# Moving 21 of 24 merge gates into the delta-net and state-space stages of a hybrid block, with convolutions in chunks and chain instructions put ahead

## The chip, the cores and the metric

The kernel runs on one core of a Trainium2 chip. The metric is the device time in microseconds of one execution. TensorE (PE) multiplies matrices and writes to PSUM; VectorE (DVE), ScalarE (ACT) and GpSimd (POOL) work on elements; SyncE (SP) issues most of the DMAs. Each engine takes its instructions in the order in which they stand in its own queue, and waits at an instruction until its inputs are there and its output buffer is free.

## The reference, cut to what matters

The kernel computes one layer of a hybrid block on 1024 tokens (plus 16 learned ones put in front, so T = 1040) and a model width of 1024. Three branches read the same normed input; three gates, each as wide as the model, weigh their projections:

```
u = rmsnorm(h, norm1_w) @ w_in                 # q, k, v, gate, b, a | z, x, B, C, dt | q, k, v | 3 x 1024 gate columns
y_gdn = gdn_branch(...)      # silu(conv4(q, k, v)), l2 norm, delta rule in chunks, rmsnorm * silu(gate); 8 heads of 128
y_ssd = ssd_branch(...)      # silu(conv4(x, B, C) + bias), chunked scan, skip, silu(z), rmsnorm per group; 4 groups
y_swa = swa_branch(...)      # window of 128, 16 query heads, sinks
g_a, g_b, g_c = split(sigmoid(gate_logits))
merged = g_a * (y_gdn @ w_proj_gdn) + g_b * (y_ssd @ w_proj_ssd) + g_c * (y_swa @ w_proj_swa)
h = h + merged @ w_out
h = h + square(relu(rmsnorm(h, norm2_w) @ w_up)) @ w_down
out = rmsnorm(h, final_norm_w)[:, 16:]
```

`conv4` is a causal convolution over four tokens, one set of four weights for each channel. All of it is computed to fp32 accuracy.

## The kernel before, in words

Each big matrix product is three matmuls: weights and activations are split into a rounded part and a rest (`hnh` and `hnl` for the normed input, `kh` and `kl` for a weight), and high x high, high x low and low x high are added up in PSUM. A weight of 1024 x 128 is loaded by SP, rounded by ACT (L118) and its rest computed by POOL (L120). `gemm` (L144) then runs 3 x 8 matmuls for each chunk of columns, two chunks of 512 for a gate, or three of 348, 346 and 346 columns where the 16 extra tokens are needed. Its PSUM tiles come from three buffers of the tag `mm`.

The stages stand one behind the other: norm, delta net (eight heads), state space (four groups), attention, merge, output projection, MLP. In the delta net a head h is worked in three phases that overlap across heads. First come projections and convolutions for q, k and v. `conv_steps` copies three chunks from PSUM into `raw` on ACT (L344), then makes the four taps on DVE over all 1040 columns (a TENSOR_SCALAR on L348 or L350, three SCALAR_TENSOR_TENSOR on L353), then silu (tanh on ACT L355, DVE L356). Second, the products: `ktp` and `vtp` are transposes, `kk` and `kk0` (L434, L440) multiply k with k, DVE scales them to `w` (L437), `kq` multiplies q with k and DVE scales it to `dm` (L473), `qtp` (L480) transposes q; the two sets of decay factors are made by ACT (L423, L427) from a tile `gm` that arrives by DMA. Third, the serial part: the triangular system is solved in steps between DVE, ACT and PE (`lq`, `lu`, `lt`), and then nine chunks are scanned. One scan step is a chain through three engines: `ks` (PE, L583) to `rr` (DVE, L585) to `py` (PE, L591) to `y` (ACT, L593) to `psn` (PE, L598) to `S` (DVE, L603), and again `ks`; `po` (L608, L609) makes the output. `gdn_final` norms that output and transposes it (`yf`, L633).

The serial part is woven into projections. `weave` sets a generator, `gemm` calls `tick` after each matmul, and after as many columns as the generator named last (`WL, WR, WY, WS`) the generator's next step is emitted. What is left when the projections of a phase are out is emitted by `drain` without any filler. The order on the engines is not just the order of this text: a scheduler places instructions by its own model of time, and `high_priority` lets an instruction be placed ahead of others that are ready.

The state-space groups run in `stage_ssd`: B, C and two x tiles are projected and convolved; `xtp` transposes x, DVE multiplies it by dt (`xd`, L715), POOL makes `xw` (L720), `st` (L756) multiplies it with B. z is projected for the output gate. The group before is finished in the meantime: `ssd_stats` sums squares (`sst`, L803, `sf`, L808), `ssd_row` transposes the factors (`sfr`, L813) and stores them, and `ssd_norm` loads them back over all partitions (`fb`, L821), multiplies (L824) and stores the branch's result in DRAM (`yd`).

In the merge, for b in three branches and m in eight output tiles, a gate is projected (`mgm`), passed through tanh, and kept in a tile; then the branch is projected (`pr`, L1059) and DVE multiplies and adds. Two gates are made beside attention, and the third at the start; within the merge the gate two places ahead is emitted before each projection. The 16 tiles of a branch's `y` are loaded and split (`yr`, `yh` L131, `yl` L132) at m = 0.

Of the kernel before, what the change touches and what calls it, by code (L numbers as in the profile page):

```python
# [53 lines left out]
WL, WR, WY, WS = 1800, 3200, 2000, 2200  # L54
# [6 lines left out]
class Trunk:  # L61
# [275 lines left out]
    def conv_steps(self, wt, tag, wcol, bcol, name):  # L337
        nc = self.nc
        raw = self.bt("raw", name + "raw", [P, T + 3])
        ths = [self.bt("th", name + "th", [P, 528]) for _ in HALVES]  # L340
        dst = self.bt(tag, name + "2")
        nc.gpsimd.memset(raw[:, 0:3], 0.0)
        for c0, n, ps in self.proj(wt, CH_ALL, name):
            nc.scalar.activation(raw[:, 3 + c0:3 + c0 + n], ps, AF.Copy)  # L344
            yield
        w = lambda j: self.cols[:, wcol + j:wcol + j + 1]
        if bcol is None:
            nc.vector.tensor_scalar(dst, raw[:, 0:T], w(0), None, op0=ALU.mult)  # L348
        else:
            nc.vector.tensor_scalar(dst, raw[:, 0:T], w(0), self.cols[:, bcol:bcol + 1],  # L350
                                    op0=ALU.mult, op1=ALU.add)
        for j in range(1, 4):
            nc.vector.scalar_tensor_tensor(dst, raw[:, j:j + T], w(j), dst, op0=ALU.mult, op1=ALU.add)  # L353
        for th, (a, b) in zip(ths, HALVES):
            nc.scalar.activation(th[:, 0:b - a], dst[:, a:b], AF.Tanh, scale=0.5)  # L355
            nc.vector.scalar_tensor_tensor(dst[:, a:b], th[:, 0:b - a], 1.0, dst[:, a:b],  # L356
                                           op0=ALU.add, op1=ALU.mult)
        return dst
# [35 lines left out]
    def gdn_kr(self, st):  # L394
# [35 lines left out]
        for c0 in (1, 5):  # L430
            ps = self.pb("kk")
            for j in range(4):
                a = cs(c0 + j)
                nc.tensor.matmul(ps[:, j * P:(j + 1) * P], k2[:, a:a + P], k2[:, a:a + P], start=True, stop=True)  # L434
            for j in range(4):
                c = c0 + j
                nc.vector.scalar_tensor_tensor(w[:, c - 1, :], ps[:, j * P:(j + 1) * P], nbk[:, c:c + 1],  # L437
                                               dm[:, c - 1, :], op0=ALU.mult, op1=ALU.mult)
# [10 lines left out]
    def gdn_vr(self, s):  # L449
        nc, vsc, v2 = self.nc, s["vsc"], s["v2"]  # L450
        vt = self.bt("vt", "vt", [P, NC, P])
        for c0, m, ps in self.to_tok(v2, "vtp"):
            nc.vector.tensor_tensor(vt[:, c0:c0 + m, :], ps,
                                    vsc[:, c0:c0 + m].unsqueeze(2).broadcast_to([P, m, P]), op=ALU.mult)
        s["vt"] = vt
# [5 lines left out]
    def gdn_qr(self, st):  # L461
        nc, q2, qt, k2, dm, bk = self.nc, st["q2"], st["qt"], st["k2"], st["dm"], st["bk"]
        s = lambda nm, w=NC: self.sm.tile([P, w], F32, name=nm)
        nc.gpsimd.tensor_tensor(qt.rearrange("p c t -> p (c t)"), qt.rearrange("p c t -> p (c t)"),
                                q2[:, META:T], op=ALU.mult)
        for c0 in (1, 5):
            ps = self.pb("kq")
            for j in range(4):
                a = cs(c0 + j)
                nc.tensor.matmul(ps[:, j * P:(j + 1) * P], k2[:, a:a + P], q2[:, a:a + P], start=True, stop=True)  # L470
            for j in range(4):
                c = c0 + j
                nc.vector.scalar_tensor_tensor(dm[:, c - 1, :], ps[:, j * P:(j + 1) * P], bk[:, c:c + 1],  # L473
                                               dm[:, c - 1, :], op0=ALU.mult, op1=ALU.mult)
        psq = s("psq", NC)
        for c0 in (1, 5):
            ps = self.pb("qtp")
            for j in range(4):
                a = cs(c0 + j)
                nc.tensor.transpose(ps[:, j * P:(j + 1) * P], q2[:, a:a + P], self.ident)  # L480
# [46 lines left out]
    def gdn_levels(self, s):  # L527
# [8 lines left out]
        for b in (0, 2):  # L536
# [4 lines left out]
            nc.scalar.copy(q[hi:hi + 32, :, 0:32], v(ps, hi, hi + 32, 32))  # L541
        yield WL
        ps = self.pc("lu")
        for b in (0, 2):
# [4 lines left out]
            nc.scalar.copy(u[lo:hi, :, hi:hi + 32], v(ps, lo, hi, 32))  # L549
# [5 lines left out]
        nc.scalar.copy(tt[32:64, :, 0:32], v(ps, 32, 64, 32))  # L555
# [6 lines left out]
        nc.scalar.copy(q[64:128], v(ps, 64, 128, 64))  # L562
# [5 lines left out]
        nc.scalar.copy(u[0:64, :, 64:128], v(ps, 0, 64, 64))  # L568
        yield WL

    def gdn_scan(self, s):
# [4 lines left out]
        for c in range(NC):  # L576
# [4 lines left out]
            else:  # L581
# [3 lines left out]
                nc.vector.scalar_tensor_tensor(rr, ps[:, 0:P], self.neg[:, c, h:h + 1], vt[:, c, :],  # L585
                                               op0=ALU.mult, op1=ALU.add)
# [6 lines left out]
            nc.scalar.copy(y[0:n], ps[0:n, 0:P])  # L593
            yield WY
            So = S
            if c < NC - 1:
# [3 lines left out]
                if c == 0:  # L600
                    nc.vector.tensor_copy(S2, ps[:, 0:P])
                else:
                    nc.vector.scalar_tensor_tensor(S2, S, self.egl[:, h, c:c + 1], ps[:, 0:P],  # L603
                                                   op0=ALU.mult, op1=ALU.add)
                S = S2
            if c > 0:
# [3 lines left out]
                nc.scalar.copy(vt[:, c, :], ps[:, 0:P])  # L610
                sqo = self.sm.tile([P, P], F32, name="sqo", bufs=1)
                nc.scalar.activation(sqo, ps[:, 0:P], AF.Square, accum_out=ms[:, c - 1:c])
# [24 lines left out]

    def stage_gdn(self, cur):
        nc = self.nc
        prev = old = None  # L640
        for h in range(GH):
# [16 lines left out]
        self.gdn_gate(prev)  # L658
        self.drain()
# [181 lines left out]
    def stage_ssd(self):  # L841
        prev = None
        for g in range(SG):
# [23 lines left out]
            self.ssd_feat(st, 0)  # L867
            prev = st
# [176 lines left out]

    def merge_load(self, b):
        place = lambda n: self.half("y", 4 * KT, n)
        self.y = [[self.split_half(self.yd[b][k][:, 512 * c:512 * c + 512], "y", place, self.nc.vector)
                   for c in range(2)] for k in range(KT)]
# [22 lines left out]
    def stage_merge(self, w2):  # L1072
        self.mg = {}
        seq = [(b, m) for b in range(3) for m in range(KT)]
        for i, (b, m) in enumerate(seq):
# [4 lines left out]
            self.merge_proj(b, m)  # L1080

# [147 lines left out]
def build(ctx, tc, I, out):  # L1229
# [6 lines left out]
    with nc.allow_non_contiguous_dma(reason="layout"):  # L1236
# [25 lines left out]
        k.lp = pool(ctx, "lp", reuse_waits="tile")  # L1262
        k.stage_merge(w2)
        ph.close()
# [77 lines left out]
```

## Time and profile before

| what | us |
|---|---|
| median of 3 runs (2763.79 to 2771.05) | 2766.74 |
| profiled execution | 2763.2 |
| its span | 2761.5 |
| norm and first projections | 0 to 90 |
| delta net | 90 to 720 |
| state space | 720 to 1119 |
| attention with two gates | 1119 to 1422 |
| merge | 1422 to 1925 |
| output projection and MLP | 1925 to 2761.5 |

The span runs from the first to the last instruction of the profiled execution; 1.7 us of the execution lie outside. The stages' ends are read from the timeline and overlap somewhat, since the next stage's projections fill the last head's scan. In the views below, a group of instructions is printed as line, engine, operation, output <- inputs, shapes and count; behind the bar stand busy time, mean duration in ns, and the idle time of the engine in front of these instructions with what ended it. A waiting engine that is not TensorE costs nothing by itself.

### The profile page before, as it was taken

The page shows a single profiled execution, that of the slowest core. Times are in us where ns is not written, and L with a number is a line of the kernel's source. Part 1 is how long each engine was busy: PE and PEld are TensorE (multiplying, and loading weights), DVE is VectorE, ACT ScalarE, POOL GpSimd, SP SyncE. Part 2 cuts the span into 40 slices and gives each one's busy share as a digit, 9 for nine tenths or more (in the row PEclk, how much of TensorE's full clock was granted, in tenths as well). Part 3 has the DMA queues.
Part 4 walks back from the last instruction along what each step waited for, and adds up shares of the span by engine and source line. Part 5 has one row for each costly group of instructions (what it writes and reads, how often), then busy time and mean ns, then how long its engine had stood idle before and what let it go on. Part 6 is the DMA issues. An engine that isn't in the chain of part 4 may idle for free.

```text
span 2761.5 us, 36981 instructions
## 1 busy us (share of the span) xinstructions
PE 2629.8 (95%) x14367; PEld 2234.7 (81%) x14367; DVE 1456.6 (53%) x2775; ACT 906.1 (33%) x2385; POOL 696.3 (25%) x519
## 2 busy tenths in 40 slices
PE   6998999999999999999999999999999999999998
PEld 5887888888898898788878888888778777777776
DVE  5777766775665765576750122424254544444445
ACT  4434444443332332465541121212442121212122
POOL 3222222221232332322112222222432222222220
PEclk9989999998999999999999999999999999999999
DMA  3211121111112111322131131313221111111101
GB/s 120 64 42 53 52 60 52 53 44 49 47 62 85 62 62 62 88 61 63 47 122 46 54 106 46 107 53 114 90 73 54 39 53 44 50 47 51 47 16 69
DMA packets 88366, 172.94 MB, mean 63 GB/s; under 512 B 35862, under 2 KB 36278, under 8 KB 88190
## 3 DMA queue, kind: packets, MB, share of 16 engines
q1 hardware_dynamic: 83982, 162.81, 18.3%
q0 software_dynamic: 3200, 6.43, 1.1%
q8 instruction: 113, 1.85, 0.3%
q10 hardware_dynamic: 1008, 1.34, 0.1%
q14 instruction: 63, 0.52, 0.1%
HBM read 144.96 MB, written 19.14 MB: 59 GB/s over the span
## 4 chain that ended last, share of the span: by engine, by line
PE 75%; DVE 17%; issue 3%; ACT 2%; DMA 2%; POOL 1%; DVEq 0%; SPq 0%; POOLq 0%; ACTq 0%
PE up L144 13%; PE dn L1177 11%; PE mgm L144 9%; PE pr L1059 9%; PE pso L1108 3%; PE x L144 3%; PE gg L144 2%; PE aq L144 2%; PE v L144 2%; DVE xt L508 2%; PE z L144 2%; PE b L144 2%; PE q L144 1%; PE c L144 1%; PE k L144 1%
## 5 line engine op out<-in xcount | busy, mean ns | idle before, releaser
L1179 DVE SCALAR_TENSOR_TENSOR h<-dn,rs,h 128x512 f32<-128x512 f32 x256 | 191.9, 750 | 132.7 <-PE dn L1177 132.7
L1177 PE MATMUL dn<-wdh,ah 128*128 128x512 f32 x512 | 203.9, 398 | 14.9 <-DVE h L1179 14.9
L1161 DVE TENSOR_TENSOR ra<-ra 128x512 f32<-128x512 f32 x64 | 94.4, 1475 | 214.2 <-ACT ra L1160 214.2
L1177 PE MATMUL dn<-wdh,al 128*128 128x512 f32 x512 | 202.3, 395 | 0.0
L1177 PE MATMUL dn<-wdl,ah 128*128 128x512 f32 x512 | 202.2, 395 | 0.0
L1059 PE MATMUL pr<-yl,wph 128*128 128x512 f32 x384 | 150.1, 391 | 1.9 <-DVE yl L132 1.9
L1059 PE MATMUL pr<-yh,wph 128*128 128x512 f32 x384 | 150.1, 391 | 1.8 <-ACT wph L118 1.0
L132 POOL TENSOR_TENSOR wdl<-wdr,wdh 128x512 fp32r<-128x512 f32 x64 | 81.9, 1308 | 274.9 <-PE dn L1177 273.5
L1059 PE MATMUL pr<-yh,wpl 128*128 128x512 f32 x384 | 149.5, 389 | 0.0
L120 POOL TENSOR_TENSOR wul<-wur,wuh 128x1024 fp32r<-128x1024 f32 x32 | 76.6, 2393 | 249.7 <-PE up L144 246.7
L1177 PEld LDWEIGHTS dn<-wdh,ah 128*128 128x128 f32 x512 | 96.1, 188 | 45.6 <-DVE h L1179 23.9
L144 PE MATMUL up<-ul,wuh 128*128 128x512 f32 x512 | 129.0, 394 | 0.0
L144 PE MATMUL up<-uh,wul 128*128 128x512 f32 x512 | 128.4, 391 | 0.0
L144 PE MATMUL up<-uh,wuh 128*128 128x512 f32 x512 | 128.2, 391 | 0.0
L1069 DVE SCALAR_TENSOR_TENSOR gt<-gt,pr 128x512 f32<-128x512 f32 x32 | 21.9, 687 | 198.9 <-PE pr L1059 198.9
L131 ACT ACTIVATE wdh<-wdr 128x512 fp32r<-128x512 f32 x64 | 40.5, 633 | 255.5 <-PE dn L1177 246.6
L120 POOL TENSOR_TENSOR wpl<-wpr,wph 128x1024 fp32r<-128x1024 f32 x24 | 61.2, 2549 | 228.2 <-ACT wph L118 205.3
L1177 PEld LDWEIGHTS dn<-wdh,al 128*128 128x128 f32 x512 | 96.2, 188 | 23.3
L1177 PEld LDWEIGHTS dn<-wdl,ah 128*128 128x128 f32 x512 | 96.2, 188 | 21.8
L144 PEld LDWEIGHTS up<-ul,wuh 128*128 128x128 f32 x512 | 96.9, 190 | 20.0
L144 PEld LDWEIGHTS up<-uh,wul 128*128 128x128 f32 x512 | 96.4, 188 | 19.7
L144 PEld LDWEIGHTS up<-uh,wuh 128*128 128x128 f32 x512 | 96.1, 188 | 20.1
(422 smaller groups left out, 6563.2 us busy)
## 6 DMA issues: line engine op xcount, KB each, us to landing
wur<-in_wup SPq DMA_DIRECT2D x32, 512.0 KB
wdr<-in_wdn SPq DMA_DIRECT2D x64, 256.0 KB
mgr<-in_win SPq DMA_DIRECT2D x24, 512.0 KB
wpr<-in_wpr SPq DMA_DIRECT2D x24, 512.0 KB
yr<-yd SPq DMA_DIRECT2D x48, 256.0 KB
dms<-rowd SPq DMA_DIRECT2D x16, 512.0 KB
wor<-in_wout SPq DMA_DIRECT2D x32, 256.0 KB
gm<-rowd SPq DMA_DIRECT2D x8, 576.0 KB
```

The source lines that it names most:

```text
L120: nc.gpsimd.tensor_tensor(wl, wr, wh.bitcast(F32), op=ALU.subtract)
L131: nc.scalar.activation(h, r, AF.Copy)
L132: eng.tensor_tensor(l, r, h.bitcast(F32), op=ALU.subtract)
L144: nc.tensor.matmul(ps[:, 0:n], a[:, k, :], b[k][:, c0:c0 + n], start=(i == 0 and k == 0), stop=(i == 2 and k == KT - 1))
L508: nc.vector.tensor_tensor(tv, lb[:, j:j + 1, j + 1:32].broadcast_to([3 * n_, n, m]), ub[:, 0:n, j:j + 1].broadcast_to([3 * n_, n, m]), op= ...
L1059: nc.tensor.matmul(ps, x[:, k, :], y, start=(k == 0 and j == 0), stop=(k == KT - 1 and j == 2))
L1069: nc.vector.scalar_tensor_tensor(t, t, 1.0, ps, op0=ALU.add, op1=ALU.mult)
L1108: nc.tensor.matmul(ps, x[k, th][:, ts], y, start=(k == 0 and j == 0), stop=(k == KT - 1 and j == 2))
L1161: nc.vector.tensor_tensor(r, r, r, op=ALU.mult)
L1177: nc.tensor.matmul(ps, a[:, ts], b, start=(j == 0 and i == 0), stop=(j == G - 1 and i == 2))
L1179: nc.vector.scalar_tensor_tensor(self.h2[t][:, qs], ps, self.rs[:, t:t + 1], self.h2[t][:, qs], op0=ALU.mult, op1=ALU.add)
```

## The change

The change has four parts.

1. 21 of the 24 gates, all behind (0, 2), are no longer made in the merge. `gate_spill` projects a gate (`mgs`), applies tanh into a tile `gs` and stores it to DRAM (`gad`); it is called once or twice for each head of delta net, four times before the last scan, and once in the state-space groups 1 and 3. `gate_load` loads a gate's two halves, two places ahead.
2. The columns between two chain steps grow from 1800, 3200, 2000, 2200 to 2800, 4900, 3050, 3400.
3. A convolution is made in three chunks, as its projection delivers them; the last tap (and the bias) is made by ACT straight from PSUM (L348 in the new numbering), the other three and the silu by DVE on the chunk.
4. Chain instructions on DVE and ACT (`w`, `vt`, `dm`, the solve's copies, `rr`, `y`, `S`, `po`'s copies) are emitted at high priority.

Besides, the merge loads the next branch's `y` at m = 4, the middle branch into space that the normed input has left. The number of matmuls and their columns do not change.

```diff
-WL, WR, WY, WS = 1800, 3200, 2000, 2200
+WL, WR, WY, WS = 2800, 4900, 3050, 3400
+SPILLED = tuple((b, m) for b in range(3) for m in range(KT) if (b, m) > (0, 2))
...
         for c0, n, ps in self.proj(wt, CH_ALL, name):
+            d = dst[:, c0:c0 + n]
             nc.scalar.activation(raw[:, 3 + c0:3 + c0 + n], ps, AF.Copy)
+            if bcol is None:
+                nc.scalar.activation(d, ps, AF.Copy, scale=w(3))
+            else:
+                nc.scalar.activation(d, ps, AF.Identity, scale=w(3), bias=self.cols[:, bcol:bcol + 1])
+            for j in range(3):
+                nc.vector.scalar_tensor_tensor(d, raw[:, c0 + j:c0 + j + n], w(j), d, op0=ALU.mult, op1=ALU.add)
+            th = self.bt("th", name + "th", [P, 528])[:, 0:n]
+            nc.scalar.activation(th, d, AF.Tanh, scale=0.5)
+            nc.vector.scalar_tensor_tensor(d, th, 1.0, d, op0=ALU.add, op1=ALU.mult)
             yield
...
-                nc.vector.scalar_tensor_tensor(rr, ps[:, 0:P], self.neg[:, c, h:h + 1], vt[:, c, :],
-                                               op0=ALU.mult, op1=ALU.add)
+                with self.tc.high_priority():
+                    nc.vector.scalar_tensor_tensor(rr, ps[:, 0:P], self.neg[:, c, h:h + 1], vt[:, c, :],
+                                                   op0=ALU.mult, op1=ALU.add)
...
+    def gate_spill(self, n=1):
+        nc = self.nc
+        for _ in range(n):
+            b, m = self.todo.pop(0)
+            for c0, k, ps in self.gemm(self.gate_w(b, m), (self.hnh, self.hnl), CH_REAL, "mgs"):
+                t = self.tp.tile([P, 512], F32, name="gs", tag="t", bufs=4)
+                nc.scalar.activation(t, ps, AF.Tanh, scale=0.5)
+                nc.sync.dma_start(self.gad[KT * b + m, :, c0 - META:c0 - META + k], t)
...
                 self.weave(self.gdn_tail(prev))
                 self.gdn_gate(prev)
+                self.gate_spill()
             self.gdn_solve(cur)
             self.gdn_vr(cur)
             self.gdn_q(cur)
+            self.gate_spill()
...
-            if m == 0:
-                self.merge_load(b)
-            if i < len(seq) - 2:
-                self.merge_gates(seq[i + 2][0], (seq[i + 2][1],), w2 if i == 0 else None)
+            if i == 0:
+                self.y = self.merge_load(0)
+                self.merge_gates(0, (2,), w2)
...
+            elif i < len(seq) - 2:
+                self.gate_load(*seq[i + 2])
             self.merge_proj(b, m)
+            if m == KT // 2 and b < 2:
+                ynext = self.merge_load(b + 1)
```

How the scheduler then places the instructions can be read from the order on each engine. Head 0 of delta net comes first. On TensorE before, where its k is transposed (`ktp`) and multiplied with itself (`kk`, `kk0`; `k_320` is head 0's k), and `k` and `v` without a number are the next head's projections:

```order
L375 MATMUL ktp<-ident,k_320 128x128
L144 MATMUL k<-hnh,kh 128x348 x2
L434 MATMUL kk<-k_320 128x128 x8
L144 MATMUL k<-hnh,kh 128x348
L144 MATMUL k<-hnl,kh 128x348 x8
...
L144 MATMUL v<-hnl,vh 128x348 x8
L144 MATMUL v<-hnh,vl 128x348 x6
L440 MATMUL kk_784<-k_320 32x32
```

And on TensorE now, at the same place:

```order
L145 MATMUL q<-hnh,ql 128x346 x2
L374 MATMUL ktp<-ident,k_318 128x128 x9
L433 MATMUL kk<-k_318 128x128 x8
L440 MATMUL kk_806<-k_318 32x32
L374 MATMUL vtp<-ident,v_360 128x128 x9
L145 MATMUL mgs<-hnh,mgh 128x512 x8
```

The projections of the next head that lay between `kk` and `kk0` (87 matmuls in twelve rows) have moved behind a gate, which is behind `vtp`. On ACT now, the taps of head 0's q (L348, which read PSUM) stand behind two sets of decay factors:

```order
L402 ACTIVATE jk,pss<-kt 128x128
L417 ACTIVATE qt<-gm 128x1024
L422 ACTIVATE dm<-dm,ngam 128x128 x8
L426 ACTIVATE dm_1441<-dm_1441,ngam 32x32
L348 ACTIVATE q_945<-q,cols 128x348
L348 ACTIVATE q_945<-q,cols 128x346 x2
```

Before, only L344 read q's PSUM tiles, ahead of all of these. The second place is one and a half steps of a middle head's scan on TensorE, with the next head's q as filler. Before:

```order
L583 MATMUL ks<-S,k_1022 128x128
L144 MATMUL q<-hnl,qh 128x346 x4
L591 MATMUL py<-rr,w 128x128
L144 MATMUL q<-hnh,ql 128x346 x3
L598 MATMUL psn<-y,kt 128x128
L608 MATMUL po<-S,qt 128x128
L609 MATMUL po<-y,dm 128x128
L144 MATMUL q<-hnh,ql 128x346
```

And now:

```order
L590 MATMUL ks<-S,k_1115 128x128
L145 MATMUL q<-hnh,ql 128x346 x8
L145 MATMUL q<-hnh,qh 128x346 x7
L599 MATMUL py<-rr,w 128x128
L145 MATMUL q<-hnh,qh 128x346
L145 MATMUL q<-hnl,qh 128x346 x8
L607 MATMUL psn<-y,kt 128x128
L618 MATMUL po<-S,qt 128x128
L619 MATMUL po<-y,dm 128x128
L145 MATMUL q<-hnh,ql 128x346 x8
L145 MATMUL mgs<-hnh,mgh 128x512 x2
```

Each link of the chain now has 9 to 15 matmuls beside it, where it had 1 to 4. The third place is the start of the second state-space group. On TensorE before, `xtp` (transposes of x) is followed by z's projection, and `st` comes some twelve rows later:

```order
L144 MATMUL x<-hnh,xl 128x346 x8
L375 MATMUL xtp<-ident,x_8428 128x128 x8
L144 MATMUL z<-hnh,zh 128x512 x2
L375 MATMUL xtp<-ident,x_8428 128x128
L144 MATMUL z<-hnh,zh 128x512 x6
L144 MATMUL z<-hnl,zh 128x512 x8
```

And now:

```order
L145 MATMUL x<-hnh,xl 128x346 x8
L374 MATMUL xtp<-ident,x_9934 128x128 x9
L781 MATMUL st<-xw,btk 128x128
L145 MATMUL z<-hnh,zh 128x512 x8
L145 MATMUL z<-hnl,zh 128x512 x8
```

One `st` has moved ahead of the z projection. On DVE at this place, the norm of the group before (L824, now L849, which reads the loaded `fb`) stood behind `xd`; now it stands ahead of it:

```order
L840 COPY sfr<-sfr 8x128
L849 SCALAR_TENSOR_TENSOR x_9116<-x_9116,hnw,fb 128x1024
L849 SCALAR_TENSOR_TENSOR x_9253<-x_9253,hnw,fb 128x1024
L740 TENSOR_TENSOR xd<-xtp,dt_539 128x512 x2
L740 TENSOR_TENSOR xd<-xtp,dt_539 128x128
```

So `xd`, which `xw` and `st` need, is now behind two instructions that wait for a DMA.

More of the change, by code (lines that the diff above doesn't have):

```diff
@@ L452, in gdn_vr @@
         for c0, m, ps in self.to_tok(v2, "vtp"):
-            nc.vector.tensor_tensor(vt[:, c0:c0 + m, :], ps,
-                                    vsc[:, c0:c0 + m].unsqueeze(2).broadcast_to([P, m, P]), op=ALU.mult)
+            with self.tc.high_priority():
+                nc.vector.tensor_tensor(vt[:, c0:c0 + m, :], ps,
+                                        vsc[:, c0:c0 + m].unsqueeze(2).broadcast_to([P, m, P]), op=ALU.mult)
         s["vt"] = vt
@@ L472, in gdn_qr @@
                 c = c0 + j
-                nc.vector.scalar_tensor_tensor(dm[:, c - 1, :], ps[:, j * P:(j + 1) * P], bk[:, c:c + 1],
-                                               dm[:, c - 1, :], op0=ALU.mult, op1=ALU.mult)
+                with self.tc.high_priority():
+                    nc.vector.scalar_tensor_tensor(dm[:, c - 1, :], ps[:, j * P:(j + 1) * P], bk[:, c:c + 1],
+                                                   dm[:, c - 1, :], op0=ALU.mult, op1=ALU.mult)
         psq = s("psq", NC)
@@ L540, in gdn_levels @@
                                  tt[lo:hi, c, 0:32], start=True, stop=True)
-            nc.scalar.copy(q[hi:hi + 32, :, 0:32], v(ps, hi, hi + 32, 32))
+            with self.tc.high_priority():
+                nc.scalar.copy(q[hi:hi + 32, :, 0:32], v(ps, hi, hi + 32, 32))
         yield WL
@@ L548, in gdn_levels @@
                                  u[hi:hi + 32, c, hi:hi + 32], start=True, stop=True)
-            nc.scalar.copy(u[lo:hi, :, hi:hi + 32], v(ps, lo, hi, 32))
+            with self.tc.high_priority():
+                nc.scalar.copy(u[lo:hi, :, hi:hi + 32], v(ps, lo, hi, 32))
         yield WL
@@ L554, in gdn_levels @@
                              q[32:64, c, 0:32], start=True, stop=True)
-        nc.scalar.copy(tt[32:64, :, 0:32], v(ps, 32, 64, 32))
+        with self.tc.high_priority():
+            nc.scalar.copy(tt[32:64, :, 0:32], v(ps, 32, 64, 32))
         yield WL
@@ L561, in gdn_levels @@
         q = self.bt("qs", "qs2", [P, NB, 64])
-        nc.scalar.copy(q[64:128], v(ps, 64, 128, 64))
+        with self.tc.high_priority():
+            nc.scalar.copy(q[64:128], v(ps, 64, 128, 64))
         yield WL
@@ L567, in gdn_levels @@
                              start=True, stop=True)
-        nc.scalar.copy(u[0:64, :, 64:128], v(ps, 0, 64, 64))
+        with self.tc.high_priority():
+            nc.scalar.copy(u[0:64, :, 64:128], v(ps, 0, 64, 64))
         yield WL
@@ L592, in gdn_scan @@
             y = self.sm.tile([P, P], F32, name="y")
-            nc.scalar.copy(y[0:n], ps[0:n, 0:P])
+            with self.tc.high_priority():
+                nc.scalar.copy(y[0:n], ps[0:n, 0:P])
             yield WY
@@ L599, in gdn_scan @@
                 S2 = self.sm.tile([P, P], F32, name="S")
[L600 to L604, printed above, removed]
+                with self.tc.high_priority():
+                    if c == 0:
+                        nc.vector.tensor_copy(S2, ps[:, 0:P])
+                    else:
+                        nc.vector.scalar_tensor_tensor(S2, S, self.egl[:, h, c:c + 1], ps[:, 0:P],
+                                                       op0=ALU.mult, op1=ALU.add)
                 S = S2
@@ L609, in gdn_scan @@
                 nc.tensor.matmul(ps[:, 0:P], s["dm"][:, c - 1, :], y, start=False, stop=True)
-                nc.scalar.copy(vt[:, c, :], ps[:, 0:P])
+                with self.tc.high_priority():
+                    nc.scalar.copy(vt[:, c, :], ps[:, 0:P])
                 sqo = self.sm.tile([P, P], F32, name="sqo", bufs=1)
-                nc.scalar.activation(sqo, ps[:, 0:P], AF.Square, accum_out=ms[:, c - 1:c])
+                with self.tc.high_priority():
+                    nc.scalar.activation(sqo, ps[:, 0:P], AF.Square, accum_out=ms[:, c - 1:c])
             yield WS
@@ L1044, in merge_gates, with gate_load @@
                 self.gates[m, (c0 - META) // 512] = t
+    def gate_load(self, b, m):
+        for c in range(2):
+            t = self.gates[m, c] = self.tp.tile([P, 512], F32, name="gt", tag="t", bufs=4)
+            self.nc.sync.dma_start(t, self.gad[KT * b + m, :, 512 * c:512 * c + 512])
     def merge_load(self, b):
-        place = lambda n: self.half("y", 4 * KT, n)
-        self.y = [[self.split_half(self.yd[b][k][:, 512 * c:512 * c + 512], "y", place, self.nc.vector)
-                   for c in range(2)] for k in range(KT)]
+        place = lambda n: self.half("y", 4 * KT, n, pool=self.y2 if b == 1 else self.lp)
+        return [[self.split_half(self.yd[b][k][:, 512 * c:512 * c + 512], "y", place, self.nc.vector)
+                 for c in range(2)] for k in range(KT)]
     def merge_proj(self, b, m):
```

32 lines of the change are left out of this document (16 added, 16 removed).

## The prediction

> **What bounds the kernel now.** I read the page first: busy time by engine, the slices, and the shares of the chain.
>
> ```profile
> PE 2629.8 (95%) x14367; PEld 2234.7 (81%) x14367; DVE 1456.6 (53%) x2775; ACT 906.1 (33%) x2385; POOL 696.3 (25%) x519
> PEclk9989999998999999999999999999999999999999
> PE 75%; DVE 17%; issue 3%; ACT 2%; DMA 2%; POOL 1%; DVEq 0%; SPq 0%; POOLq 0%; ACTq 0%
> ```
>
> TensorE is busy for 95% of 2761.5 us, so no change that keeps its work can win more than what it loses in gaps, at half clock and in stalls. The 17% of DVE in the chain say where the gaps are: in stages where a chain alternates between the two engines. The second view is the table of windows by stage (us, PE, PEld, DVE, ACT and POOL busy, granted clock, DMA share, GB/s).
>
> ```profile
> 90.00:221.00 131.00, 119.04 (x770) 106.26 (x769) 96.62 (x242) 53.36 (x176) 40.02 (x29) 0.93 0.22 63
> 221.00:640.00 419.00, 388.27 (x2879) 352.09 (x2879) 291.63 (x722) 179.82 (x592) 107.13 (x73) 0.98 0.18 52
> 640.00:720.00 80.00, 73.20 (x490) 63.73 (x489) 42.06 (x94) 30.69 (x108) 16.01 (x14) 0.89 0.16 50
> 720.00:1119.00 399.00, 380.63 (x2331) 349.40 (x2331) 255.52 (x288) 125.13 (x273) 128.05 (x75) 0.97 0.20 65
> 1119.00:1422.00 303.00, 295.80 (x1838) 249.94 (x1837) 201.61 (x695) 163.61 (x643) 66.65 (x123) 1.00 0.23 65
> 1450.00:1925.00 475.00, 475.00 (x2073) 389.09 (x2072) 118.46 (x123) 95.48 (x133) 107.85 (x45) 1.00 0.23 75
> ```
>
> The rows are: heads 0 and 1 of delta net, its middle heads, its last head, state space, attention, merge. The merge is the stretch without any loss: 475.00 busy of 475.00, 229 ns for each of 2073 matmuls. A gate is 48 matmuls there, so 11.0 us. Delta net and state space lose 12.0, 30.7, 6.8 and 18.4 us in gaps (length less PE busy). The clock adds to that: one minus the granted clock, times the length, is 9, 8, 9 and 12 us. The sums are 21, 39, 15.5 and 30.5 us, 106 us in all. This is the ground on which the change plays. What the gaps of the middle heads wait for stands in the groups of that window (behind the bar: busy, mean ns, idle before and its releaser):
>
> ```profile
> L591 PE MATMUL py<-rr,w 128*128 128x128 f32 x86 | 18.6, 298 | 17.5 <-DVE rr L585 17.5
> L480 PE MATMUL qtp<-ident,q 128*128 128x128 f32 x40 | 8.5, 350 | 9.9 <-DVE dm L473 9.9
> L583 PE MATMUL ks<-S,k 128*128 128x128 f32 x88 | 18.1, 287 | 1.7 <-DVE S L603 1.7
> L585 DVE SCALAR_TENSOR_TENSOR rr<-ks,neg,vt 128x128 f32<-128x128 f32 x43 | 15.0, 348 | 17.3 <-PE ks L583 17.2
> ```
>
> py of the scan waits 17.5 us for rr, which itself takes 0.348 us: the wait is not rr, but what stands ahead of it on DVE.
>
> **The change part by part.**
>
> *Moved gates.* 21 gates of 11.0 us, 231 us of TensorE, go from a stretch without loss to the stages with losses. By themselves they change nothing; only the 106 us can shrink, and new stalls can come. Storing and loading 21 x 512 KB adds 10.5 MB each way at some 60 GB/s of present traffic; I cost it at nothing, hidden by a DMA share of 0.16 to 0.23.
>
> *Middle heads (h = 2 to 7), +26 us.* In the order a scan step had mostly four matmuls of 346 columns between ks and py, now 15. Between po and ks there was one, now ten. The wait for rr came from long instructions of DVE:
>
> ```profile
> L353 DVE SCALAR_TENSOR_TENSOR k<-kraw,cols,k 128x1040 f32<-128x1040 f32 x15 | 23.5, 1564 | 0.3
> L353 DVE SCALAR_TENSOR_TENSOR q<-qraw,cols,q 128x1040 f32<-128x1040 f32 x15 | 19.4, 1295 | 0.0
> L348 DVE TENSOR_SCALAR v<-vraw,cols 128x1040 f32<-128x1040 f32 x5 | 13.1, 2628 | 12.0 <-ACT vraw L344 12.0
> L344 ACT ACTIVATE qraw<-q 128x346 f32<-128x346 f32 x11 | 5.1, 463 | 0.6 <-PE q L144 0.6
> ```
>
> A chain instruction could stand behind 1.3 to 2.6 us. A third of 1040 columns is about 0.5 us (estimate: 1295/3 plus a fixed part), and the chain's own are put ahead. ACT takes the fourth tap: 3 x 0.46 = 1.4 us per convolution, 40 convolutions, 55 us on an engine that is 33% busy; hidden, unless it stands ahead of a chain copy, where it costs 0.5 us. I count 16 of the 17.5 us of py, the 1.7 of ks, and the 8 of the clock, whose short windows follow these gaps: 26. The 9.9 us of qtp stay, because dm's instructions still follow the norm of the former head on DVE. Bounds: 0 (the gaps are re-timed only) and 39.
>
> *Last head (640 to 720), +13 us.* Its scan had only the first state-space projections between its steps; four gates, 44 us, are added. 15.5 us are lost there, half of them at a low clock:
>
> ```profile
> 674.00:688.00 14.00, 14.00 (x79) 12.01 (x77) 0.87 (x3) 3.36 (x10) 0.75 (x4) 0.51 0.06 25
> 838.00:848.00 10.00, 9.09 (x36) 8.64 (x35) 0.45 (x2) 1.52 (x2) 1.65 (x1) 0.51 0.14 53
> ```
>
> I let 2.5 us remain. Bounds: 0 and 15.5.
>
> *Head 0 (90 to 221), -8 us.* Here filler is taken away. Before, k and v of head 1 lie between kk and kk0. Now nothing does: ktp, kk, kk0, vtp and then gates, whose PSUM buffer is freed by a tap (L348) that stands in ACT's order behind the second eight dm instructions.
>
> ```profile
> 92.05 2.05 PE L434 MATMUL kk<-k 128*128 128x128 f32 x16
> 94.10 1.43 PE L144 MATMUL k<-hnl,kh 128*128 128x348 f32 x8
> 95.37 1.43 PE L144 MATMUL k<-hnh,kl 128*128 128x348 f32 x8
> ...
> 107.89 0.25 PE L440 MATMUL kk<-k 128*32 128x32 f32 x2
> ...
> 109.43 0.82 PE L375 MATMUL vtp<-ident,v 128*128 128x128 f32 x6
> 106.72 2.15 DVE L437 SCALAR_TENSOR_TENSOR w<-kk,nbk,dm 128x128 f32<-128x128 f32 x8
> 111.51 2.46 ACT L423 ACTIVATE dm<-dm,ngam 128x128 f32<-128x128 f32 x8 [3.75 <-POOL dm L420]
> ```
>
> (First number: the start; second: the duration.) TensorE ends kk at 94.1. The tap follows 111.51 + 2.46 and the 32x32 dm, so the gate starts at about 114.8; kk0 (0.25) and vtp (9 of 0.14, as in the row of six) lie between: 19 us idle. The clock behind such a stop was 0.51 for 10 us (838 to 848): up to 5, taken as 3. Head 0's solve starts no earlier while TensorE reaches its readers with less work ahead: 5 us, which no row prices (bounds 0 and 10). Of the 21 us lost there now about 2 stay, since the waits of its first scan get fillers as in the middle heads: 27 + 2 against 21 is -8. Bounds: -27 (nothing of the old goes) and +3 (the tap comes soon after 107, when ACT is free).
>
> *State space, -8 us.* In groups 1 to 3, `st` now stands ahead of z's projection on TensorE, and on DVE two norm instructions (L824, now L849) ahead of xd. The norm waits for a load, xd for the norm, xw for xd, st for xw, and z and all behind it for st. At the end of the stage the same load is seen alone:
>
> ```profile
> 1118.76 0.27 PE L813 MATMUL sfr<-ident,sf 128*8 128x128 f32 x1 [1.44 <-POOL sf L808]
> 1124.09 3.81 DVE L824 SCALAR_TENSOR_TENSOR x<-x,hnw,fb 128x1024 f32<-128x1024 f32 x2 [4.74 <-DMA fb<-frd]
> 848.87 1.49 DVE L715 TENSOR_TENSOR xd<-xtp,dt 128x512 f32<-128x512 f32 x3 [5.77 <-PE xtp L375]
> L824 DVE SCALAR_TENSOR_TENSOR x<-x,hnw,fb x8: 1276/2222/3155, 850.3 to 1126.6; 128x1024 f32<-128x1024 f32 x8
> L720 POOL TENSOR_TENSOR xw<-xd,tail 128x1152 f32<-128x1152 f32 x8 | 21.0, 2628 | 17.0 <-DVE xd L715 16.9
> PE sst L803 <- DVE sq L801: 5.6, 4, 1.6
> PE xtp L375 <- DVE x L356: 4.3, 3, 1.5
> ```
>
> From sfr: the load 5.3, two norms of 1.3 to 2.2 (shortest and median), xd 1.5, xw 2.6: st can run at 12.0 to 13.8. TensorE has five runs of eight before it, 1.27 us each from start to start as in the rows of 94.10 and 95.37, and xtp of about 1.2: 7.5. Each group stalls 4.5 to 6.3 us, 8.2 with the longest norms; three groups, I take 17. Against it, sst (5.6) and xtp (4.3) have gates and shorter convolution steps in front: +9 of 9.9. Sum -8. Bounds: +9 (xd does not wait) and -40 (8.2 us and 5 us of low clock, three times).
>
> *Merge start and merge, -2 us.* The tiles of y that the first projection reads come as in this group of 1416 to 1450:
>
> ```profile
> L131 ACT ACTIVATE yh<-yr 128x512 fp32r<-128x512 f32 x16 | 9.7, 628 | 11.2 <-DMA yr<-yd 11.1
> ```
>
> 9.7 + 11.2 us for 16 tiles, twice the 11 us of a projection, so it waits for them in both kernels; before, part of a gate lay between. Afterwards a projection has 11 us to itself, and DVE, 118.46 of 475.00 busy, and ACT, 95.48, must serve it in half the time: still under half. Bounds: -10 and +3. Attention, output and MLP keep their orders: 0.
>
> *Two rules of the Trainium skill.* The first concerns DVE beside POOL:
>
> ```profile
> L348 DVE TENSOR_SCALAR v<-vraw,cols x8: 754/2622/2639, 66.6 to 604.3; 128x1040 f32<-128x1040 f32 x8
> L120 POOL TENSOR_TENSOR ggl<-ggr,ggh x8: 2359/2362/2383, 111.6 to 627.5; 128x1024 fp32r<-128x1024 f32 x8
> ```
>
> The same instruction of DVE takes 754 ns at its shortest and 2622 in the median; the convolution step takes 1295 or 1564 ns, while rr stays at 348. The Trainium skill, "SBUF — State Buffer", section "🔬 SBUF: two separate sides", says that DVE and GpSimd share a port pair under an exclusive lock, so that a DVE instruction with two SBUF inputs, or in a 2-port mode, waits for the whole of GpSimd's. It speaks against the change, which brings 19 weight splits of POOL into delta net; the even 348 ns of rr, one of whose inputs is PSUM, and the 2622 ns agree with it. The worst victim, the TENSOR_SCALAR, goes with the change, so I cost the rest at nothing; the other end is a rival. The second concerns the clock, at 0.51 for 14 and 10 us in the rows above. The Trainium skill, "TensorE: Matmul & The Clock Gate", section "🔬 Part 1: The HAM clock gate (the "warmup" mystery)", has the full clock back after some 3.4 us of activity; a stop would cost 1.7 us by that, and the sum would be 1 us better. The rows show three to four times as long, and they are used.
>
> **The sum.** +26 +13 -8 -8 -2 = 21 us gained. From the profiled execution, 2761.5 of span and 1.7 around it, 2763.2: 2742. The median of the runs shown, 2766.7, is 3.5 higher; 2742 lies 0.9% under it.
>
> **The rivals.**
> - *Fillers cover nearly all.* Middle heads 37, last head 15, head 0 nothing lost, state space +4: 56, so 2707. For it: py and ks now have 2 us of work in front of them. Against it: qtp's 9.9 us, whose cause stays.
> - *State space decides, slower.* The st stall is 8 us with 5 us of low clock behind it, three times, 39 us, with no gain at sst and xtp; of 39 gained in delta net, 8 and 2 go as before and another 2 to the clock in head 0: -12, so 2775. It outweighs all the rest from about 10 us for each group. For it: the row of 838 to 848 has the clock at 0.51 in just this place. Against it: the load may land while x is still projected.
> - *Re-timed only.* The middle heads' chain keeps its waits for DVE (10 gained), the last head gains 12, the losses are as forecast: +4, so 2759, which can't be told from no change. For it: DVE is busy for 70% of that window (291.63 of 419.00).
> - *The lock rules.* Each of the 19 splits holds a convolution step with a chain instruction behind it for the 2.4 us that one of 128x1024 takes on POOL: 45 us, so 2787. Against it: the 15 steps of k exceed those of q by 0.27 us only. This is the rule of the Trainium skill's "SBUF — State Buffer" taken at its worst.
>
> **How the numbers follow.** Forecast 2742 with 0.44; fillers cover all 0.16; state space decides 0.16; re-timed only 0.20; the lock 0.04. A measurement tells apart 0.3%, 8 us. Faster: 0.44 + 0.16 and a little less for the edge of the forecast, 0.59; same: 0.20 and that edge, 0.22; slower 0.19. Range 2703 to 2778: from the first rival to the second, with the lock and the far ends left out.
>
> **What would show it.** Right: in 221 to 640, py waits under 5 us for rr and the clock is 0.99 or more; at 674 no low clock; TensorE idle from about 94 to 114, ended by the gate's matmul; st L781 waiting 4 to 8 us for xw in three groups; the merge still full, now half as long. Wrong: py still waits 15 us or more (the DVE order did not matter); st without a wait (+17); a merge in which pr waits for yl or the gates' loads; or chain steps of DVE longer than 348 ns.

## The result, and the profile after

| | median us (lowest to highest) | ratio to before, 95% interval |
|---|---|---|
| before | 2766.9 (2763.8 to 2771.1), 4 runs | |
| changed | 2806.1 (2802.0 to 2808.7), 4 runs | 1.0134 (1.0113 to 1.0156) |

The changed kernel is 39 us slower, where 21 us of gain was forecast; 2806 lies above the range of 2703 to 2778, too. The two profiled executions, of 2763.2 and 2808.7 us, lie 45 us apart, 6 more than the medians; sums from the traces below come out at 45. One of the ten executions of run 4 below took 5136.6 us, which nothing here explains; what is given for that run is from the other nine. The page of the changed kernel, with the rows that answer to those shown before:

```profile
PE 2640.8 (94%) x14367; PEld 2244.5 (80%) x14367; DVE 1483.2 (53%) x3015; ACT 968.7 (35%) x2545; POOL 694.1 (25%) x519
PEclk9889999999999999998999999999999999999999
PE 78%; DVE 12%; ACT 4%; POOL 2%; DMA 2%; issue 2%; SPq 0%; POOLq 0%; DVEq 0%; ACTq 0%
```

The number of matmuls is the same, 14367. The share of DVE in the chain has fallen from 17% to 12%, as it should where a chain between TensorE and DVE gets more cover. But ACT, which was at 2%, has 4%. The windows by stage show where it went; the columns are as before, and the stages' ends have moved, since the gates now lie in the early ones:

```profile
90.00:260.00 170.00, 144.37 (x868) 127.93 (x869) 102.40 (x275) 69.81 (x213) 42.56 (x32) 0.88 0.20 63
260.00:800.00 540.00, 512.01 (x3411) 448.64 (x3410) 318.99 (x837) 222.50 (x676) 134.97 (x85) 0.99 0.20 63
800.00:912.00 112.00, 106.53 (x647) 90.04 (x646) 30.29 (x69) 39.40 (x123) 26.31 (x17) 0.98 0.23 78
912.00:1384.00 472.00, 426.64 (x2481) 388.23 (x2481) 255.93 (x389) 158.76 (x344) 132.88 (x75) 0.92 0.17 57
1699.00:1967.00 268.00, 265.34 (x1150) 214.54 (x1149) 131.03 (x138) 60.70 (x86) 60.37 (x25) 1.00 0.46 150
```

The fourth row is state space: 45.4 us of gaps (18.4 before) and a granted clock of 0.92 (0.97 before). The first is head 0: 25.6 us of gaps (12.0) at 0.88 (0.93). The last head has 5.5 us of gaps at 0.98, against 6.8 at 0.89. The merge, now projections alone, has 2.7 us of gaps; 2.5 of these are the first projection's wait for its y, and the row of before began behind that place.

Because gaps and low clock overlap, I use one more measure for comparing kernels. At a mark that every kernel has (a certain matmul of the program), I take the time and subtract the work done so far, each matmul at its own start-to-start pace at full clock (512 columns 227 ns, 346 157 ns, and so on, read from the trace of before). What is left is the time lost up to the mark, in us:

```
mark                                      before  changed   change of the loss since the mark above
end of head 0 (its last yf)                 60.9     76.7   +15.8
end of head 6                              136.9    145.7   - 7.0
end of head 7                              150.9    152.9   - 6.8
end of state space (last sfr)              206.3    252.6   +44.3
end of attention                           245.8    294.0   + 1.9
end of the merge                           257.2    301.5   - 3.9
end of the MLP                             294.5    339.7   + 0.9
```

The waits of TensorE over the whole changed kernel (engine, who waits for whom: us, times, longest) name the new ones:

```profile
PE vtp L374 <- DVE vt L454: 16.9, 7, 2.5
PE kk L440 <- DVE w L437: 14.3, 1, 14.3
PE qtp L482 <- DVE dm L475: 12.4, 7, 2.1
PE z L145 <- ACT x L350: 11.1, 3, 4.2
PE st L781 <- POOL xw L745: 9.7, 3, 3.4
PE yfs L812 <- DVE yt L804: 6.4, 3, 3.0
PE mgs L145 <- ACT q L348: 2.8, 1, 2.8
```

py, which waited 21.1 us for rr, is not among them any more. But five waits were not there before. Two were forecast: st for xw, and mgs for a convolution tap on ACT (L348). Three were not: vtp for vt in seven heads, z for another such tap (L350), and yfs for yt. That of z, in the timelines of TensorE, ACT and DVE at the start of the third group (start, duration, line, and in brackets the idle time before with its releaser):

```profile
1186.17 0.33 PE L374 MATMUL xtp<-ident,x 128*128 128x128 f32 x1 [0.35 <-DVE xd L740]
1189.67 0.48 PE L781 MATMUL st<-xw,btk 16*128 16x128 f32 x2 [3.17 <-POOL xw L745]
1194.33 3.78 PE L145 MATMUL z<-hnh,zh 128*128 128x512 f32 x8 [4.17 <-ACT x L350]
1197.91 3.21 PE L145 MATMUL z<-hnl,zh 128*128 128x512 f32 x8
...
1202.81 2.02 PE L145 MATMUL z<-hnh,zh 128*128 128x512 f32 x8
1204.67 2.02 PE L145 MATMUL z<-hnl,zh 128*128 128x512 f32 x8
1193.63 1.70 ACT L350 ACTIVATE x<-x,cols 128x348 f32<-128x348 f32 x3 [8.18 <-DMA yd<-x]
1182.54 2.48 DVE L849 SCALAR_TENSOR_TENSOR x<-x,hnw,fb 128x1024 f32<-128x1024 f32 x2 [4.89 <-DMA fb<-frd]
```

Read it from the bottom: the load fb lands, DVE norms the group before, its result is stored (`yd<-x`), and only when that store has landed may ACT write the new x into one of three tiles of the tag `kt`. That write is the fourth tap, and it reads the projection's PSUM tile; until it has run, its PSUM tile is not free, and z, the next projection, has none. The 3.2 us for xw and 4.2 us for the tap follow one another, and the first eight z matmuls then take 3.58 us from start to start, those of 1202.81 only 1.86: the granted clock was 0.53 from 1190 to 1201. Groups two and four show the same sequence: st waits 3.4 and 3.2 us for xw, then z waits 3.5 us for the tap, both times.

### The profile page after: what moved, and what is told of

Read it like the earlier page. It is cut to its first block, busy times and chain, and to the rows that moved or that the text cites. A ratio compares the mean times of both kernels' runs of the same rounds, so it can differ in the third digit from the quotient of the medians.

```text
span 2806.9 us, 37524 instructions
## 1 busy us (share of the span) xinstructions
PE 2640.8 (94%) x14367; PEld 2244.5 (80%) x14367; DVE 1483.2 (53%) x3015; ACT 968.7 (35%) x2545; POOL 694.1 (25%) x519
## 4 chain that ended last, share of the span: by engine, by line
PE 78%; DVE 12%; ACT 4%; POOL 2%; DMA 2%; issue 2%; SPq 0%; POOLq 0%; DVEq 0%; ACTq 0%
PE up L145 12%; PE dn L1218 11%; PE pr L1091 9%; PE mgs L145 6%; PE z L145 4%; PE aq L145 3%; PE gg L145 3%; PE v L145 3%; PE q L145 3%; PE x L145 3%; PE pso L1149 3%; PE k L145 2%; DVE xt L510 1%; DVE ra L1202 1%; PE b L145 1%
## 5 line engine op out<-in xcount | busy, mean ns | idle before, releaser
L121 POOL TENSOR_TENSOR wul<-wur,wuh 128x1024 fp32r<-128x1024 f32 x32 | 76.7, 2397 | 250.6 <-PE up L145 247.6
L121 POOL TENSOR_TENSOR mgl<-mgr,mgh 128x1024 fp32r<-128x1024 f32 x24 | 57.5, 2396 | 208.9 <-PE mgs L145 98.7
```

The costliest lines, as they stand in the source:

```text
L121: nc.gpsimd.tensor_tensor(wl, wr, wh.bitcast(F32), op=ALU.subtract)
```

## The experiments

**Two theories for the loss.** P: the tap that reads PSUM holds one of three PSUM tiles until its own output tile, or its place in ACT's queue, comes; in state space that is a store, in head 0 it is two sets of decay factors. N: the loss is that of the forecast's own list, the norm's load and `st`, and the tap only fills time that is idle anyway.

*Run 1, the tap reads the copy.* The only edit to the changed kernel:

```diff
+            rt = raw[:, 3 + c0:3 + c0 + n]
             if bcol is None:
-                nc.scalar.activation(d, ps, AF.Copy, scale=w(3))
+                nc.scalar.activation(d, rt, AF.Copy, scale=w(3))
             else:
-                nc.scalar.activation(d, ps, AF.Identity, scale=w(3), bias=self.cols[:, bcol:bcol + 1])
+                nc.scalar.activation(d, rt, AF.Identity, scale=w(3), bias=self.cols[:, bcol:bcol + 1])
```

> One edit to the changed kernel: ACT's fourth tap (L348, L350) reads the copy in raw instead of PSUM, so that a PSUM tile is free again after the copy, as before the change. Theory P (the tap holds one of three PSUM buffers until its own output tile or its place in ACT's queue comes): the stop at kk0 (14 us idle) gets filler, z no longer waits for the tap (11 us) and st no longer stands ahead of z (10 us), the low clock behind both goes; state space falls from 44 us more than before to under 10, head 0 from 16 to under 8, together 2806 - 40 = about 2765, or down to 2750. Theory N (the norm's load and st's place make the loss, the tap only fills what is idle anyway): state space keeps 30 us or more, 2795 to 2806.

Measured: 2757.1 us (2749.8 to 2759.4), 0.996 of before (0.9945 to 0.9974). Before took 2769.2 beside it, so one operand turns 39 us of loss into some 12 us of gain. TensorE in head 0 of this run:

```profile
92.25 1.95 PE L434 MATMUL kk<-k 128*128 128x128 f32 x16
93.96 0.94 PE L145 MATMUL mgs<-hnh,mgh 128*128 128x512 f32 x3
...
108.36 0.25 PE L441 MATMUL kk<-k 128*32 128x32 f32 x2
```

A gate runs right behind kk and the next head's k behind it. In the changed kernel nothing stood there:

```profile
106.68 0.32 PE L440 MATMUL kk<-k 128*32 128x32 f32 x2 [14.26 <-DVE w L437]
...
112.17 3.44 PE L145 MATMUL mgs<-hnh,mgh 128*128 128x512 f32 x8 [2.79 <-ACT q L348]
```

At the end of head 0 the loss is 55.2 us instead of 76.7. State space loses 69.1 (131.6 to 200.7), against 99.7 in the changed kernel and 55.4 before. The scheduler, too, sees the PSUM tile come free earlier: it puts z back in front of `st`. So the run shows what the operand costs with what it does to the order; it doesn't part the two.

*Run 2, the old convolution in state space alone.* Convolutions with a bias (B, C and x) go through the code of before; all else is the changed kernel.

```diff
     def conv_steps(self, wt, tag, wcol, bcol, name):
+        if bcol is not None:
+            return (yield from self.conv_old(wt, tag, wcol, bcol, name))
         nc = self.nc
...
```

Not printed here is `conv_old` itself, which is the convolution of before.

> The changed kernel with the convolution of before in state space only (those with a bias); delta net, gates and priorities stay. Theory P: the 44 us that state space loses go almost all, 2806 - 38 = about 2768; head 0 still stops for 14 us at kk0. Theory N, or a theory that the two gates put into groups 1 and 3 and the tight DVE are at fault: at most 10 us come back, 2796 or more.

Measured: 2766.7 us (2761.6 to 2771.6), ratio 0.9994 (0.9977 to 1.001). State space loses 57.9 us (151.8 to 209.7) and is all but as before, though the two gates are still in it: 42 of 44 us come back. So the loss came with the convolution's new form, not with the gates. The stop at kk0 is there in full:

```profile
PE kk L465 <- DVE w L462: 14.2, 1, 14.2
```

By itself this run doesn't part the two theories either. With the old convolution the scheduler also puts the norm (L874) behind xd again, and z ahead of `st`, so what N needs is gone as well. Group two of this run:

```profile
1054.77 1.49 DVE L765 TENSOR_TENSOR xd<-xtp,dt 128x512 f32<-128x512 f32 x3 [3.17 <-PE xtp L399]
1058.11 3.19 DVE L874 SCALAR_TENSOR_TENSOR x<-x,hnw,fb 128x1024 f32<-128x1024 f32 x2 [1.86 <-DMA fb<-frd]
1054.92 0.71 PE L145 MATMUL z<-hnh,zh 128*128 128x512 f32 x2
```

What decides is which wait ends last in the changed kernel. In its third group, shown above, `st` had its input and ran at 1189.67, and z started only at 1194.33, behind the tap; in groups two and four the order is the same. Without the wait of `st`, z would by this trace have started no sooner, since the tap came later. The load and the norm of theory N do take part, as links on the way to the store and the tap. But they stop z only because the tap holds the PSUM tile, and in run 1, where it does not, z runs there without a wait. Together with run 1 the loss of state space can be split: 31 us by the tap's reading PSUM, with what that does to the order (99.7 to 69.1), and 11 us that remain when the tap reads raw (69.1 to 57.9). In run 1 ACT still waits some 7 us at the tap for the store, now with a free PSUM tile, and what is behind it is late:

```profile
1158.34 1.81 ACT L351 ACTIVATE x<-xraw,cols 128x348 f32<-128x348 f32 x3 [7.14 <-DMA yd<-x]
PE yfs L813 <- DVE yt L805: 8.3, 3, 3.6
PE xtp L375 <- DVE x L356: 8.2, 6, 2.5
```

*Run 3, head 0 without its gate.*

```diff
             self.gdn_q(cur)
-            self.gate_spill()
+            if h:
+                self.gate_spill()
...
-        self.gate_spill(4)
+        self.gate_spill(5)
```

> The changed kernel, but head 0 gets no gate and the last head gets five instead of four. Theory G (the gate, put ahead of the next head's projections, is what takes the filler from kk0): the stop of 14 us goes, 2806 - 14 = about 2792. Theory P: the projection that follows then waits for the same PSUM buffer behind the same tap, the stop stays at 12 to 16 us, 2803 to 2808.

Measured: 2802.1 us (2799.6 to 2803.2), ratio 1.0127 (1.0098 to 1.0155). The stop is of the same length:

```profile
PE kk L440 <- DVE w L437: 16.5, 2, 14.3
```

It isn't the gate that pushes the filler away. What follows vtp is now k of head 1, and it needs the same PSUM tiles, which the same tap holds: k waits 2.78 us for q's tap (L348), as the gate did. The 4 us by which the median is lower are no more than executions of one kernel differ by.

*Run 4, the old convolutions everywhere,* with gates, column counts and priorities of the change.

> The changed kernel with the convolutions of before everywhere; the 21 gates as filler, the column counts and the priorities stay. Theory P: state space and head 0 lose nothing against before, so what is left is the gain of the gates alone: middle heads keep their gain only if the wait for rr came from too little filler (py under 5 us, 2740 to 2750); if it came from the long convolution steps of DVE in front of rr, py waits 15 us again and the time is 2755 to 2765. Theory N: 2795 or more.

Measured: 2756.6 us (2748.1 to 2768.3), ratio 0.9959 (0.9939 to 0.9979). py waits 2.4 us in the whole kernel, though DVE's convolution steps are as long as before:

```profile
PE py L601 <- DVE rr L595: 2.4, 6, 0.4
```

So py is free as in the first branch of the expectation, and the time is that of the second. The long steps still delay rr: in heads 1 to 6, 12 of its 48 instructions start 0.5 to 2.3 us after ks is done, each behind a convolution step. TensorE just has enough filler there to work on. Yet the middle heads gain only 5.2 us (from the end of head 0 to that of head 6: 70.8 lost, 76.0 before); vtp waits 15.6 us.

*Runs 5 and 6, priorities alone and gates alone.* Run 5 is the kernel before with the high priorities of the change. Run 6 is run 4 without them; its edit also takes out the priorities that attention has in the kernel before.

> The kernel before with the high priorities of the change alone; no gate is moved, convolutions and column counts are the old ones. If py's wait of 19.7 us came from long DVE instructions placed ahead of rr, it falls under 6 us and the time to 2750 to 2755. If it came from too little filler between ks and py, it stays at 15 us or more, 2763 to 2770.

> The moved gates and the larger column counts with the old convolutions and without the priorities. If the filler is what frees py, py waits under 6 us as in the run with old convolutions and priorities, and the time is within 5 us of its 2757; if the priorities do it, py waits 15 us or more and the time is 2765 to 2775.

Measured: 2773.2 us (2767.4 to 2782.2), ratio 1.0018 (1.0003 to 1.0034), and 2779.4 us (2767.7 to 2785.4), ratio 1.0035 (1.002 to 1.0049). Neither alone gains anything; together they gave 2757. Part of run 6's time is not the question asked: attention loses 6 us more there than in run 4, by the measure above. Its middle heads lose 10 us more than those of run 4 and 5 us more than those of before. The waits in the middle heads of run 5, then run 6 (the profiled execution of run 5 was the slowest of its ten, that of run 6 the fastest, so the kinds of waits are compared here, not the sum):

```profile
PE py L600 <- DVE rr L594: 9.9, 5, 2.2
PE ks L591 <- DVE S L614: 8.0, 6, 1.7
```

```profile
PE qtp L484 <- DVE dm L477: 16.5, 5, 3.4
PE vtp L376 <- DVE vt L456: 15.5, 6, 2.6
PE py L601 <- DVE rr L595: 2.0, 5, 0.4
```

With priorities alone py still waits 9.9 of its 17.5 us and ks more than its 1.7: there is too little filler. With filler alone py is free, but qtp waits 16.5 us for dm instead of 9.9; in run 4, with the priorities, it is 6.1. Both of my either-or expectations missed: the filler frees py, the priorities free dm, and the gain needs both.

*Run 7, both repairs:* the tap from raw in delta net, the old convolution in state space.

> The changed kernel with both repairs: the tap reads raw in delta net, and state space keeps the convolution of before. By theory P and the traces so far the two gains add up: delta net as in the run with the tap from raw (21 us less lost than in the changed kernel at the end of head 0's scan), state space as in the run with the old convolution there (58 us lost instead of 69): about 2757 - 11 = 2746, a ratio of 0.992 to before. If the gains do not add (head 0's repair only moves the loss), 2757 or more.

Measured: 2746.9 us (2743.2 to 2748.9), ratio 0.992 (0.9901 to 0.9939). The two gains add up as expected.

**What holds vtp?** In the changed kernel, DVE, POOL and TensorE in one head:

```profile
394.51 0.25 DVE L510 TENSOR_TENSOR xt<-lb,ub 99x90 f32<-99x90 f32 x1
...
395.08 2.29 DVE L510 TENSOR_TENSOR xt<-lb,ub 99x84 f32<-99x84 f32 x1
397.85 1.54 DVE L454 TENSOR_TENSOR vt<-vtp,vsc 128x512 f32<-128x512 f32 x3
394.81 2.46 POOL L121 TENSOR_TENSOR mgl<-mgr,mgh 128x1024 fp32r<-128x1024 f32 x1 [10.96 <-PE mgs L145]
398.59 0.47 PE L374 MATMUL vtp<-ident,v 128*128 128x128 f32 x1 [2.41 <-DVE vt L454]
```

An instruction of the solve, both of whose inputs are in SBUF, takes 2.29 us; the one of 394.51, a little larger, took 0.25. It ends at 397.37, 0.10 us behind the end of POOL's split of a gate's weight. vt stands behind it, and the ninth transpose waits for vt. The rule of the Trainium skill, "SBUF — State Buffer", section "🔬 SBUF: two separate sides", of an exclusive lock agrees with that to a tenth of a microsecond. 19 of these splits are what the change has moved from the merge to here. It is no single case: in the ten traces 109 steps of the solve take over 1.2 us, nearly all others under 0.7, and each of the 109 ends 0.04 to 0.12 us behind the end of a POOL instruction. Ten of them are in the changed kernel, seven behind the split of a gate's weight.

The kernel before has 15 such steps, and they stood in py's way. Of the ten waits of py for rr in its heads 1 to 6, nine have a step of 1.5 to 2.4 us between ks and rr; the tenth has a TENSOR_SCALAR of 2.65 us. One of the nine:

```profile
575.07 2.38 POOL L464 TENSOR_TENSOR qt<-qt,q 128x1024 f32<-128x1024 f32 x1 [2.00 <-DVE q L356]
575.28 2.22 DVE L508 TENSOR_TENSOR xt<-lb,ub 99x40 f32<-99x40 f32 x1
577.88 0.34 DVE L585 SCALAR_TENSOR_TENSOR rr<-ks,neg,vt 128x128 f32<-128x128 f32 x1
578.28 0.49 PE L591 MATMUL py<-rr,w 128*128 128x128 f32 x2 [1.60 <-DVE rr L585]
```

*Run 8, the split of a gate's weight on DVE,* added to run 7:

```diff
-        nc.gpsimd.tensor_tensor(wl, wr, wh.bitcast(F32), op=ALU.subtract)
+        eng = nc.vector if name == "mg" else nc.gpsimd
+        eng.tensor_tensor(wl, wr, wh.bitcast(F32), op=ALU.subtract)
```

> The run before, with the rest of a gate's weight (mgl) computed by DVE instead of POOL. Theory L (the wait of vtp for vt, 2.4 us a head, is a solve instruction of DVE with two SBUF inputs that is held for as long as POOL's split of the gate's weight runs): vtp's wait falls from about 17 to under 5 us and the time by 8 to 14 us, to 2732 to 2738, less what the added 1.1 us instructions on DVE cost in front of chain instructions. Rival (vt is late by its own place in DVE's order): vtp keeps 12 us or more, and the time stays or rises to 2750.

Measured: 2730.1 us (2714.3 to 2731.8), ratio 0.9848 (0.9822 to 0.9873). DVE does the split in half of POOL's time, and vtp's wait is down from 17.5 us (first row, run 7) to 4.8:

```profile
PE vtp L397 <- DVE vt L477: 17.5, 7, 3.1
L122 DVE TENSOR_TENSOR mgl<-mgr,mgh x24: 1215/1224/1226, 64.6 to 1571.3; 128x1024 fp32r<-128x1024 f32 x24
PE vtp L398 <- DVE vt L478: 4.8, 7, 3.0
PE qtp L506 <- DVE dm L499: 10.6, 6, 1.8
236.00:757.00 521.00, 507.33 (x3413) 445.00 (x3412) 302.44 (x841) 227.65 (x677) 107.14 (x73) 1.00 0.21 65
```

The last row is the window of the middle heads: 13.7 us of gaps and full clock, against 28.0 at 0.99 in the changed kernel. The middle heads lose 20 us less than in run 7, and 13 us is what vtp's wait has lost; which waits make up the rest was not taken apart. The time is 2 us better than the 2732 to 2738 that were expected. Of all versions this one is fastest, 1.5% under before (the ratio above) and 2.7% under the changed kernel (2730.1 / 2806.1 is 0.973).

## Why the prediction was wrong, point by point

- *State space, "-8 us": this step failed.* It measured 44. The part that was on the list came out smaller than priced: st waits 9.7 us for xw, not 17. What wasn't on it is the fourth tap. I counted it as "3 x 0.46 = 1.4 us per convolution ... hidden, unless it stands ahead of a chain copy", that is, as busy time of an engine with room. But its price is not its duration; it is how long a reader of PSUM may have to wait for the tile that it writes. z's 11.1 us for the tap and yfs's 6.4 are what the step lacked. With the gaps grew the low clock: its stretches in this stage are 71 us in sum (27 before). TensorE is busy in 56 of them (25 before), and half of the difference, some 16 us of the 44, is the price of the clock outside of gaps; the gaps make 27 (45.4 against 18.4). The sst wait, whose 5.6 us were to vanish, is still 5.6. The rival "State space decides" had the right place, the right sign and nearly the size (39 us), but put it all at `st`. The waits of `st` are 9.7 us, and each was over before the tap let z go.
- *Head 0, "-8 us": mechanism right, size off.* The idle time was forecast as 19 us, ending at 114.8 with the gate; it is 14.3 + 2.8 = 17.1, ending at 112.17. I did see there that the gate's "PSUM buffer is freed by a tap (L348) that stands in ACT's order behind" others, and didn't ask where else the same line holds a buffer. The loss is 15.8 instead of 8, because the low clock cost more than the 3 us that I took for it: stretches of 20.5, 3.4 and 17.1 us lie in this stage, 41 us in sum against 17 before. TensorE was busy in 26 of these 41 us, and half of that, 13 us, is what the clock cost outside of gaps.
- *Middle heads, "+26 us": 7 measured.* The wait for rr went, all of it, as forecast, and qtp's stayed (8.6 us). Of the 8 us of the clock some 5 came, with 10 us at low clock in place of 20. But "so I cost the rest at nothing", said of POOL's splits, failed: vtp's 14.4 us in the middle heads (6 times 2.4) are new and took back most of py's 17.5. The rival "The lock rules" priced 19 splits at 45 us and got 0.04; one split in a head holds up the chain (seven in all), not 19. Its argument against, the steps of k, looked at the convolution alone and not at the solve's instructions, which also have two SBUF inputs.
- *"The wait for rr came from long instructions of DVE": half right.* In nine of the ten waits the long instruction is a step of the solve that POOL held up, which the rows of the prediction do not show, and only some have convolution steps there as well. Shortening the convolution was not needed to end the wait: in run 4 its steps are as long as ever, rr is still late behind them, and py does not wait, because there is filler. The right sum for py thus came with a cause that was wrong in part.
- *Last head, "+13 us": 7.* The low clock at 674 is gone, as said; the stage's clock is 0.98, but 5.5 us of gaps stay.
- *Merge, "-2 us": +4.* The loads, which now bring 150 GB/s at a DMA share of 0.46, hide behind projections. Gates as filler cost nothing by themselves, as forecast.

The sum of the terms as they were measured, -15.8 + 7.0 + 6.8 - 44.3 - 1.9 + 3.9 - 0.9, is -45.2; the spans of the two profiled executions differ by 45.4. Of the signs that the prediction named, most came true: py does not wait for rr, the clock of the middle heads is 0.99, TensorE idles at kk0 until the gate, `st` waits in three groups (3.2 us each instead of 4 to 8). None of them looked at the tap.

## What to carry to other kernels

When a second instruction reads a PSUM tile, ask what its output tile waits for, not how long it runs: until then the tile is held, and TensorE's next projection with it. When filler brings weight splits along, look at which VectorE instructions with two SBUF inputs run beside POOL in the stage they move to. A scheduler that sees a buffer held will also reorder what is behind it, so one operand can change the order of a whole stage.

## What the runs showed of the hardware that was not expected

The low clock behind a short wait can cost more than that behind a long stop. In head 0 the clock fell at 94.6 for 20.5 us, most of which is the stop of 14.3 us itself; and once more at 162.9 for 17.1 us, a microsecond behind a wait of just 1.8 us (lq for tt). That this wait set it off is not shown. Two windows of the changed kernel:

```profile
106.00:115.00 9.00, 5.53 (x18) 4.18 (x19) 5.55 (x14) 4.55 (x14) 3.78 (x4) 0.50 0.31 81
163.00:180.00 17.00, 17.00 (x118) 12.65 (x118) 4.03 (x15) 3.21 (x7) 3.32 (x2) 0.50 0.13 33
```

In the first, behind the stop, TensorE is busy for 5.53 us at half clock, which costs some 3 us (an estimate: half of it). In the second it is busy for 17.00 of 17.00 us and has half its clock throughout, some 8.5 us by the same estimate. The Trainium skill, "TensorE: Matmul & The Clock Gate", section "🔬 Part 1: The HAM clock gate (the "warmup" mystery)", gives some 3.4 us of activity until the full clock; this trace doesn't agree, and what counts as activity there stays open.

Subtracting two SBUF tiles of 128x1024 took 2.46 us on POOL (the row of 394.81) and 1.22 us on DVE (run 8).
